# The norms of a two-layer block: weights split ahead, a fixed order of products and filler, modulation products one chunk later

## The chip, the cores and the metric

The kernel runs on one core of a Trainium2 chip. Its engines are TensorE (PE: matrix products, with PEld for its weight loads), VectorE (DVE), ScalarE (ACT), GpSimd (POOL) and SyncE (SP, which here issues the DMA loads). Each engine takes its instructions from its own queue in program order and waits at semaphores for the others. The metric is the device time of one execution in microseconds (us).

## The reference

256 tokens of width 1024 go through a first block (retention, a long convolution, a mixture of 32 experts) and then through a second block of two layers. Only the second block is touched. One layer of it is, with `rms` a root-mean-square norm over the width and six modulation vectors `sh1 ... gt2` taken from `silu(c) @ ada_w` ("ada" below):

```python
sh1, sc1, gt1, sh2, sc2, gt2 = ada_params(c, ada_w[l], ada_b[l])
h  = rms(x, g1[l]) * (1 + sc1) + sh1
u  = h @ w_in[l]               # 1024 x 2304: attention, gating, Fourier and
                               # differential-attention parts
y  = concat(fourier(u), neighbourhood_attention(u), sgu(u),
            diff_post(diff_attention(u)))   # each 256 wide, with context keys
x  = x + gt1 * (y @ w_out[l])
h  = rms(x, g2[l]) * (1 + sc2) + sh2
x  = x + gt2 * (square(relu(h @ ff1[l])) @ ff2[l])   # 1024 -> 4096 -> 1024
```

`diff_post` is a norm over each head's 64 columns. The keys and values of the context (256 tokens, computed beside the first block) also need `hc @ w_in[1]` for layer 1.

## The kernel before

Every float32 product with a large weight is done as three products of rounded halves: a weight unit of 128x1024 is split by ACT (`wh`, the rounded part) and DVE (`wl`, the rest) in `split_w` (line 277), the activations likewise (`hh`, `hl`), and PE multiplies hh by wh, hl by wh and hh by wl. `lin` (line 288) walks over a 1024x512 weight chunk in four units of two rows of tiles (k), splitting each unit just ahead of its products. A chunk lies in two buffers of 1 MB, each loaded by SP as soon as an earlier user has let the buffer go. There are seven buffers for split halves. The weights of the feed-forward come in eight chunks for `ff1` and eight for `ff2`; `ff` (line 1666) runs `ff1` of chunk c+1 before `ff2` of chunk c. After every `lin` of layer 0's feed-forward `bg_step` lets one step of "background" work in, on the modulation vectors of layer 1: two 1 MB loads of weights and 16 recorded `pada` products.

In the second block x lies transposed (`xt`). A norm is `norm_t` (line 377) and `modulated_t` (line 396): ACT squares x by pairs of tiles (`sq`), PE sums the squares with products against a column of ones (`sm,sq`), DVE takes the reciprocal root (`rq`, `sm`), PE broadcasts it over the partitions (`ident,sm`), DVE multiplies x by it (`xr`), ACT and DVE scale and shift (`hh`, `xf`) and DVE forms the rest (`hl`). Three such norms are concerned: layer 0's second norm (before its feed-forward), layer 1's first norm (computed at the end of layer 0), and layer 1's second norm. So that PE has something to do during a norm, layer 0 keeps two products of context keys back, `ctx_keys` (line 1503): 16 products `hc,w` each, whose result is copied by ACT (`ck`) and sent on. They are the "filler".

Within a layer `mixer` (line 1544) follows the string `MIX`, one letter per step: 0 to 3 are the four input projections, n and d start parts of the two attentions, b finishes the oldest started part, p is a step of the output projection `proj` (line 1595), whose last step ends with the adds into x. In layer 0 the step 0 also calls `turn` (in `layer`, line 1763), which scales x and transposes it into `xt` with 16 PE transposes and four ACT copies `x<-xt`. The last finishing step is `diff_post` (line 1466) of the last heads: a product `ones,dsq`, a reciprocal root on DVE, a copy `rb`, two transposes, a multiply (`do`) and the split `yh`. Where no order is written out by hand, a scheduler orders instructions by its own estimates; `behind` and the list `hold` pin single ones.

## Time and profile before

| what | value |
| --- | --- |
| median of 3 runs | 1798.84 us (1796.55 to 1802.67) |
| the profiled execution | 1801.79 us, its span 1800.0 us |
| mean granted clock of PE | 0.977 |
| PE busy | 1680.0 us, 93% of the span |
| DVE busy | 964.1 us, 54% |
| ACT busy | 727.0 us, 40% |
| DMA | 495.82 MB, 275 GB/s on the mean |

The second block begins at about 1092 us. Layer 0's mixer ends at 1231, its second norm lasts to 1245, its feed-forward to 1450; layer 1's first norm ends at 1463, its mixer at 1597, its second norm at 1605, its feed-forward at 1790. A busy share close to 100% says that the engine sets the time there; what is left are the stretches in which PE waits, and those in which the granted clock is 0.50, that is 1.2 instead of 2.4 GHz, where the same products take longer. In the profile a product of full float32 (filler, squares, `ones,dsq`) shows two records per instruction.

### The profile page before, as it was taken

To read this page: it belongs to the slowest core of one execution; us is meant where nothing else is said; L and a number is where in the kernel's file an instruction comes from. 1 tells how busy PE (TensorE), PEld (TensorE's weight loads), DVE (VectorE), ACT (ScalarE), POOL (GpSimd) and SP (SyncE) were. 2 spreads that over 40 slices of the span, in tenths; PEclk is the share of its full clock that TensorE was granted. 3 is DMA by queue.
4 is the path that set the end of the run, shared out by engine and by line. 5 is a ranking of instruction groups with operands and counts; after the bars stand their busy time and mean duration, and the time that the engine had idled before them with its cause. 6 is when DMAs were issued, how large, how long until landed. Compare 5 with 4: busy or idle time off the path is not lost.

```text
span 1800.0 us, 31105 instructions
## 1 busy us (share of the span) xinstructions
PE 1680.0 (93%) x12928; PEld 1323.4 (74%) x12928; DVE 964.1 (54%) x1719; ACT 727.0 (40%) x1257; POOL 62.2 (3%) x104
## 2 busy tenths in 40 slices
PE   5999999999898889999999888998999999989998
PEld 1678766668575556877677657777899987779998
DVE  5625556466224345544455466774545556755555
ACT  2413434343233333332233235563444455645443
POOL 0000000000000000000000001010000000100000
PEclk9999999999999999999999998999999999989999
DMA  9654578967699999899989995624877736235551
GB/s 372 269 211 164 225 294 324 354 243 272 277 420 420 421 396 394 319 408 420 420 350 420 403 399 162 212 96 136 299 267 257 258 126 202 80 118 188 190 189 44
DMA packets 79059, 495.82 MB, mean 275 GB/s; under 512 B 8928, under 2 KB 15744, under 8 KB 22464
## 3 DMA queue, kind: packets, MB, share of 16 engines
q1 hardware_dynamic: 74496, 478.30, 69.7%
q0 software_dynamic: 3152, 10.47, 2.0%
q10 hardware_dynamic: 1264, 4.98, 0.7%
q8 instruction: 104, 1.70, 0.4%
q14 instruction: 43, 0.35, 0.1%
HBM read 486.91 MB, written 6.82 MB: 274 GB/s over the span
## 4 chain that ended last, share of the span: by engine, by line
PE 63%; DVE 4%; ACT 3%; DMA 2%; issue 2%; DVEq 0%; ACTq 0%
PE pf L200 23%; PE pm L200 19%; PE acc L200 11%; PE pa L200 5%; PE pj L200 2%; PE pm L203 1%; DVE wl L209 1%; DMA w<-in_e 1%; PE pf L203 1%; PE pada L200 1%; DMA w<-in_ada_w 1%; ACT wh L206 0%; ACT e L206 0%; DVE sm L1320 0%; DMA w<-in_w_out 0%
## 5 line engine op out<-in xcount | busy, mean ns | idle before, releaser
L209 DVE TENSOR_TENSOR wl<-w,wh 128x1024 fp32r<-128x1024 f32 x346 | 422.9, 1225 | 421.8 <-PE pa L200 107.9
L206 ACT ACTIVATE wh<-w 128x1024 fp32r<-128x1024 f32 x346 | 362.7, 1057 | 416.6 <-PE pa L200 171.8
L200 PE MATMUL pf<-hh,wh 128*128 128x256 f32 x592 | 168.3, 286 | 4.0 <-ACT hh L206 2.3
L200 PE MATMUL pf<-hl,wh 128*128 128x256 f32 x592 | 167.1, 284 | 2.5 <-DVE hl L209 2.5
L200 PE MATMUL pf<-hh,wl 128*128 128x256 f32 x592 | 165.4, 285 | 1.6 <-DVE wl L209 1.5
L200 PE MATMUL acc<-hh,wh 128*128 128x256 f32 x512 | 143.6, 280 | 0.0
L200 PE MATMUL acc<-hl,wh 128*128 128x256 f32 x512 | 143.0, 279 | 0.0
L200 PE MATMUL acc<-hh,wl 128*128 128x256 f32 x512 | 142.9, 279 | 0.0
L200 PE MATMUL pm<-w,xg 128*32 128x256 f32 x2048 | 132.3, 390 | 2.3 <-ACT sm L206 1.2
L200 PEld LDWEIGHTS pf<-hh,wh 128*128 128x128 f32 x592 | 112.8, 191 | 8.7 <-issue 3.3
L200 PEld LDWEIGHTS pf<-hl,wh 128*128 128x128 f32 x592 | 112.7, 190 | 5.6 <-DVE hl L209 3.2
L200 PEld LDWEIGHTS pf<-hh,wl 128*128 128x128 f32 x592 | 111.8, 191 | 3.4 <-DVE wl L209 2.5
L200 PEld LDWEIGHTS pm<-w,xg 128*32 128x32 f32 x2048 | 66.7, 112 | 51.6 <-issue 13.5
L200 PEld LDWEIGHTS acc<-hh,wh 128*128 128x128 f32 x512 | 96.4, 188 | 5.9 <-ACT wh L206 5.0
L200 PEld LDWEIGHTS acc<-hh,wl 128*128 128x128 f32 x512 | 96.7, 189 | 0.0
L200 PEld LDWEIGHTS acc<-hl,wh 128*128 128x128 f32 x512 | 96.4, 188 | 0.0
L200 PE MATMUL pada<-w,csil 128*32 128x512 f32 x576 | 85.6, 625 | 9.5 <-DMA w<-in_ada_w 7.1
L200 PE MATMUL pm<-w,ex 128*32 128x256 f32 x1024 | 63.5, 388 | 16.7 <-issue 15.6
L200 PE MATMUL pm<-hh,wl 128*128 128x256 f32 x256 | 72.2, 282 | 0.0
L200 PE MATMUL pm<-hl,wh 128*128 128x256 f32 x256 | 72.2, 282 | 0.0
L200 PE MATMUL pm<-hh,wh 128*128 128x256 f32 x256 | 72.1, 282 | 0.0
L200 PE MATMUL pf<-wl,hh 128*128 128x512 f32 x160 | 65.2, 408 | 0.0
(515 smaller groups left out, 3469.9 us busy)
## 6 DMA issues: line engine op xcount, KB each, us to landing
w<-in_e SPq DMA_DIRECT2D x192, 1024.0 KB, 12.0
w<-in_ff SPq DMA_DIRECT2D x96, 1024.0 KB, 5.2
w<-in_ada_w SPq DMA_DIRECT2D x72, 1024.0 KB, 7.2
w<-in_w_in SPq DMA_DIRECT2D x54, 1024.0 KB, 7.2
w<-in_w_out SPq DMA_DIRECT2D x16, 1024.0 KB, 7.0
w<-in_ret_w_o SPq DMA_DIRECT2D x4, 1024.0 KB, 5.6
w<-in_w_su SPq DMA_DIRECT2D x3, 1024.0 KB, 4.8
adab<-in_ada_b SPq DMA_DIRECT2D x9, 256.0 KB, 12.6
```

Of the source, the lines that this page charges most:

```text
L200: return self.nc.tensor.matmul(out, lhsT, rhs, start=start, stop=stop, skip_group_check=True)
L203: return self.nc.tensor.transpose(out, in_, self.ident)
L206: return self.nc.scalar.activation(out, in_, f, **k)
L209: return self.nc.vector.tensor_tensor(out, a, b, op=op)
```

## The change

Five edits, all in the second block:

1. `ahead` splits the first two units of the weights that follow each of the three norms (`ff1` chunk 0 in both layers, the first chunk of `w_in` of layer 1) before the norm begins; `lin` takes them as ready. The DVE half of the second unit is pinned behind the last add into x, the third unit behind the last square (ACT) and behind the reciprocal root (DVE), the fourth behind the last `hl`.
2. The filler is cut into parts and each part is pinned to a place: in layer 0's second norm 3 products behind `ones,dsq` of `diff_post`, 3 behind its transposes, 4 behind the last product of squares, 6 behind the broadcast; in layer 1's first norm 4 and 12. Layer 1's second norm has none, as before.
3. The step letter `x` issues the loads of the filler and hands it to `diff_post`.
4. `turn` has a letter of its own, `t`, and runs after the projections 0, 1 and 2 instead of after 0.
5. `bg_n = -0.99, bg_rate = 1.13`: of the eight background steps in layer 0's feed-forward none runs after chunk 0, one after each of chunks 1 to 6, two after chunk 7.

```diff
-MIX = "012nndd3nbbbdndbbbvbndfdbnnsbnpbgdbdbbbbbp"
+MIX = "012nndtd3nbbbdndbbbvbndfdbnnsbnpbgdbdxbbbbbp"
...
         if self.hold:
             for later, earlier in zip(i, self.hold.pop(0)):
-                self.behind(later, earlier)
+                if earlier:
+                    self.behind(later, earlier)
         return hi, lo
 
+    def ahead(self, chunk):
+
+        self.hold = [(), (None, self.added)]
+        return chunk, [self.split_w(chunk[:, o:o + 1024]) for o in (0, 1024)]
+
     def lin(self, chunk, nk, n, jobs):
 
+        chunk, ready = chunk if isinstance(chunk, tuple) else (chunk, [])
...
-            hi, lo = self.split_w(chunk[:, u * per * n:(u + 1) * per * n])
+            hi, lo = ready[u] if u < len(ready) else self.split_w(chunk[:, u * per * n:(u + 1) * per * n])
...
-    def norm_t(self, x):
+    def norm_t(self, x, fill):
...
         rs = self.rsqrt(r, m, 2, 32.0)
+        last = self.filled(fill, last)
         p = self.ps()[:, :256]
         for t in range(2):
-            self.mm(p[:, t * P:(t + 1) * P], r[:, t:t + 1].to_broadcast([P, P]), self.ident, t == 0, True)
+            i = self.mm(p[:, t * P:(t + 1) * P], r[:, t:t + 1].to_broadcast([P, P]), self.ident, t == 0, True)
+            if t == 0 and fill:
+                self.behind(i, last)
+        self.filled(fill, i)
         return p, sq, rs
+
+    def filled(self, fill, i):
+
+        f = next(fill, None) if fill else None
+        if f:
+            self.behind(f[0], i)
+        return f[1] if f else i
...
-                if k + i == 0:
-                    self.hold = [(sq, self.added)] + [(hi, rs)] * 3
...
-            self.tt(lhs.lo[:, k:k + n, :], f, lhs.hi[:, k:k + n, :], ALU.subtract)
+            lo = self.tt(lhs.lo[:, k:k + n, :], f, lhs.hi[:, k:k + n, :], ALU.subtract)
+        self.hold = [(sq, rs), (hi, lo)]
...
+        fill = self.gap if col == 7 and not self.fill else None
+        last = self.filled(fill, i)
         r = self.rstd_of(p[:, 0:4], 4, 64.0)
...
+            if t == 0 and fill:
+                self.behind(i, last)
+        self.filled(fill, i)
...
             if step == "0":
-                self.lin(self.chunk(W[0]), 8, 512, [WJob(lhs, self.two_w(npad, nk))])
+                self.lin(w or self.chunk(W[0]), 8, 512, [WJob(lhs, self.two_w(npad, nk))])
+            elif step == "t":
                 late()
+            elif step == "x":
+                next(fill or iter(()), None)
+                self.gap = fill
...
-        lhs = self.modulated_t(xt, normed(mid), *self.mod_cols(st, self.c2("g2", 8, 8 * l), 0, 3))
-        self.bg_rate = 1.0
-        self.ff(l, xt, lhs, st[1][:, 0, 5, :])
+        w = self.ahead(self.chunk(self.a["ff1_2"][l][0]))
+        lhs = self.modulated_t(xt, self.norm_t(xt, mid), *self.mod_cols(st, self.c2("g2", 8, 8 * l), 0, 3))
+        self.bg_n, self.bg_rate = -0.99, 1.13
+        self.ff(l, xt, lhs, st[1][:, 0, 5, :], w)
         self.bg_rate = 0.0
         if not l:
-            self.norm = normed(end)
+            next(end)
+            w = self.ahead(self.chunk(self.a["w_in_2"][1][0]))
+            self.norm = self.norm_t(xt, end), w
...
-                keys = (self.ctx_keys(0, hc_d, lambda t: self.load(kv_d[1][:, :512], t.rearrange("p c k -> p (c k)"))),
-                        self.ctx_keys(1, hc_d, lambda t: self.planes(t, kd_d[1])))
+                keys = (self.ctx_keys(0, hc_d, lambda t: self.load(kv_d[1][:, :512], t.rearrange("p c k -> p (c k)")), (3, 3, 4, 6)),
+                        self.ctx_keys(1, hc_d, lambda t: self.planes(t, kd_d[1]), (4, 12)))
```

How the instructions stand before and after, at three places. A row is a line of the kernel, an operation and its tiles, out<-in, with the number of a buffer; x4 means four in a row.

PE at layer 0's second norm, before: the last output product `pj`, squares (`sm,sq`), filler (`hc,w`), broadcast (`ident,sm`), first product of the feed-forward (`hh,wh`).

```order
L200 MATMUL pj_11364<-yh_10440,wl_11708 128x256
L200 MATMUL pm_11771<-sm_11772,sq_11774 128x1 x4
L200 MATMUL pm_11816<-hc_11769,w_11767 128x256 x5
L200 MATMUL pm_11771<-sm_11772,sq_11780 128x1 x4
L200 MATMUL pm_11771<-sm_11772,sq_11786 128x1 x4
L200 MATMUL pm_11771<-sm_11772,sq_11792 128x1 x2
L200 MATMUL pm_11771<-sm_11772,sq_11796 128x1 x2
L200 MATMUL pm_11816<-hc_11769,w_11767 128x256 x11
L200 MATMUL pf_11813<-ident_81,sm_11801 128x128 x2
L200 MATMUL pf_11882<-hh_11838,wh_11884 128x256
```

The same place after the change:

```order
L200 MATMUL pj_11364<-yh_10440,wl_11719 128x256
L200 MATMUL pf_11790<-sm_11791,sq_11793 128x1 x4
L200 MATMUL pf_11790<-sm_11791,sq_11799 128x1 x4
L200 MATMUL pf_11790<-sm_11791,sq_11805 128x1 x4
L200 MATMUL pf_11790<-sm_11791,sq_11811 128x1 x2
L200 MATMUL pf_11790<-sm_11791,sq_11815 128x1 x2
L200 MATMUL pf_11569<-hc_11511,w_11509 128x256 x4
L200 MATMUL pm_11836<-ident_81,sm_11820 128x128 x2
L200 MATMUL pf_11569<-hc_11511,w_11509 128x256 x6
L200 MATMUL pf_11890<-hh_11850,wh_11782 128x256
```

The squares' products now stand together, the filler that is left stands 4 before the broadcast and 6 behind it (6 more of its 16 are further up, in `diff_post`).

DVE in the same norm, before, from the end of the reciprocal root (`sm<-rq,rq`) on:

```order
L222 SCALAR_TENSOR_TENSOR sm_11801<-rq_11803,rq_11804 128x2
L209 TENSOR_TENSOR xr_11840<-x_83,pf_11813 128x256
L219 TENSOR_SCALAR xf_11841<-xr_11840,sm_11836,adac_102 128x256
L209 TENSOR_TENSOR xr_11846<-x_83,pf_11813 128x256
L209 TENSOR_TENSOR hl_11839<-xf_11841,hh_11838 128x256
L209 TENSOR_TENSOR xr_11852<-x_83,pf_11813 128x512
L209 TENSOR_TENSOR wl_11913<-w_11878,wh_11912 128x1024
L219 TENSOR_SCALAR xf_11853<-xr_11852,sm_11836,adac_102 128x256
L209 TENSOR_TENSOR xr_11860<-x_83,pf_11813 128x512
L209 TENSOR_TENSOR hl_11839<-xf_11847,hh_11838 128x256
L209 TENSOR_TENSOR wl_11941<-w_11880,wh_11940 128x1024
L219 TENSOR_SCALAR xf_11861<-xr_11860,sm_11836,adac_102 128x256
```

After the change:

```order
L222 SCALAR_TENSOR_TENSOR sm_11820<-rq_11822,rq_11823 128x2
L209 TENSOR_TENSOR wl_11941<-w_11780,wh_11940 128x1024
L209 TENSOR_TENSOR xr_11852<-x_83,pm_11836 128x256
L219 TENSOR_SCALAR xf_11853<-xr_11852,sm_11848,adac_102 128x256
L209 TENSOR_TENSOR xr_11858<-x_83,pm_11836 128x256
L209 TENSOR_TENSOR hl_11851<-xf_11853,hh_11850 128x256
L209 TENSOR_TENSOR xr_11864<-x_83,pm_11836 128x512
L219 TENSOR_SCALAR xf_11865<-xr_11864,sm_11848,adac_102 128x256
L209 TENSOR_TENSOR xr_11872<-x_83,pm_11836 128x512
L209 TENSOR_TENSOR hl_11851<-xf_11859,hh_11850 128x256
L219 TENSOR_SCALAR xf_11873<-xr_11872,sm_11848,adac_102 128x256
L209 TENSOR_TENSOR xr_11880<-x_83,pm_11836 128x512
```

The third unit's `wl` stands in front of the first `xr`, and no other `wl` stands between the norm's own instructions.

SP's loads there, before: `ff1` chunk 0, a pair of modulation weights, `ff1` chunk 1 on both sides of the context keys' way out (`kv_d<-ck`) and of the second filler's input (`hc`), then layer 1's keys and values (`kvc`) and the next modulation pair.

```order
L225 DMA w_12009<-in_ada_w 128x2048
L225 DMA w_12011<-in_ada_w 128x2048
L225 DMA w_12027<-in_ff_2 128x2048
L225 DMA kv_d_89<-ck_11833 128x512
L225 DMA hc_13976<-hc_d 128x2048
L225 DMA w_12029<-in_ff_2 128x2048
L225 DMA kvc_14046<-kv_d_89 128x1536
L225 DMA w_12155<-in_ada_w 128x2048
L225 DMA w_12157<-in_ada_w 128x2048
L225 DMA w_12167<-in_ff_2 128x2048
```

After the change:

```order
L225 DMA w_12012<-in_ff_2 128x2048
L225 DMA w_12014<-in_ff_2 128x2048
L225 DMA w_12143<-in_ada_w 128x2048
L225 DMA w_12145<-in_ada_w 128x2048
L225 DMA kv_d_89<-ck_11845 128x512
L225 DMA hc_13976<-hc_d 128x2048
L225 DMA kvc_14058<-kv_d_89 128x1536
L225 DMA w_12155<-in_ff_2 128x2048
L225 DMA w_12157<-in_ff_2 128x2048
L225 DMA w_12273<-in_ff_2 128x2048
```

`ff1` chunk 1 stands where the first modulation pair stood, that pair stands in front of `kv_d<-ck`, and behind `kvc` come the weights of `ff2` chunk 0 (w_12155, w_12157) and not a second modulation pair. At the turn of x the 16 transposes now stand together behind the second score product after projection 2 and in front of projection 3's first product; the four copies stand on ACT behind the two exponentials that follow those scores. The instructions of POOL and of the whole first block stand as before.

## Rows read from the trace of the kernel before

**Rows 1.** waits of PE, 1222 to 1480 us: total us, times, longest

```profile
PE pa L200 <- DVE hl L209: 2.6, 3, 1.0
PE pada L200 <- DMA w<-in_ada_w: 2.6, 1, 2.6
PE pada L200 <- issue: 2.3, 1, 2.3
PE pa L200 <- ACT hh L206: 1.5, 1, 1.5
PE pf L200 <- DVE hl L209: 1.3, 1, 1.3
PE pf L200 <- ACT hh L206: 1.1, 1, 1.1
PE pj L200 <- ACT yh L206: 1.1, 1, 1.1
PE pf L203 <- DVE rb L1475: 0.6, 1, 0.6
```

**Rows 2.** busy us by stretch: PE, PEld, DVE, ACT, POOL, PEclk, DMA share, GB/s

```profile
1231.30:1238.30 7.00, 7.00 (x50) 6.57 (x49) 3.71 (x12) 2.82 (x5) 0.00 (x0) 1.00 0.00 1
1238.30:1241.70 3.40, 3.40 (x10) 2.64 (x9) 0.68 (x6) 0.00 (x0) 0.00 (x0) 0.50 0.00 0
...
1269.00:1272.40 3.40, 3.40 (x17) 2.01 (x10) 0.30 (x1) 0.00 (x0) 0.00 (x0) 0.50 1.02 424
...
1450.90:1461.40 10.50, 10.50 (x66) 9.70 (x66) 3.59 (x13) 2.14 (x4) 0.00 (x0) 1.00 0.01 2
...
1600.10:1613.80 13.70, 9.46 (x42) 8.78 (x42) 11.41 (x28) 9.06 (x16) 0.00 (x0) 0.50 0.24 79
```

**Rows 3.** timeline of PE, layer 1's first norm, its filler: start us, us, tile

```profile
1456.18 5.43 PE L200 MATMUL pf<-hc,w 128*128 128x256 f32 x24
```

**Rows 4.** timeline of PE, layer 1's second norm [idle before <-releaser]

```profile
1597.06 4.07 PE L200 MATMUL pf<-sm,sq 128*128 128x1 f32 x32
1603.02 1.22 PE L200 MATMUL pm<-ident,sm 128*128 128x128 f32 x4 [1.90 <-DVE sm L222]
...
1609.99 0.58 PE L200 MATMUL pf<-hl,wh 128*128 128x256 f32 x1 [1.20 <-DVE hl L209]
```

**Rows 5.** timeline of ACT, layer 0's second norm

```profile
1243.82 0.60 ACT L206 ACTIVATE ck<-pm 128x512 f32<-128x512 f32 x1 [9.40 <-PE pm L200]
1244.72 0.60 ACT L206 ACTIVATE hh<-xr,adac,sm 128x256 fp32r<-128x256 f32 x1 [0.30 <-DVE xr L209]
```

**Rows 6.** the page's costliest groups: count, busy us, mean ns, idle before

```profile
L209 DVE TENSOR_TENSOR wl<-w,wh 128x1024 fp32r<-128x1024 f32 x346 | 422.9, 1225 | 421.8 <-PE pa L200 107.9
```

**Rows 7.** timeline of DVE, layer 0's second norm

```profile
1252.01 0.69 DVE L209 TENSOR_TENSOR xr<-x,pf 128x512 f32<-128x512 f32 x1 [1.77 <-DMA kv_d<-ck]
```

**Rows 8.** timeline of DVE, layer 1's second norm

```profile
1604.28 0.42 DVE L209 TENSOR_TENSOR xr<-x,pm 128x256 f32<-128x256 f32 x1 [1.31 <-PE pm L200]
```

**Rows 9.** timeline of PE, the turn of x

```profile
1112.46 1.28 PE L203 MATMUL xt<-ident,x 128*128 128x128 f32 x8 [0.77 <-ACT pad L206]
1114.51 0.38 PE L200 MATMUL pa<-hh,wh 128*128 128x256 f32 x1 [0.78 <-ACT x L206]
```

**Rows 10.** timeline of PE, projection 3's first product, behind the scores

```profile
1140.95 0.58 PE L200 MATMUL pa<-wh,hh 128*128 128x512 f32 x1
```

**Rows 11.** timeline of ACT, the second exponential of those scores

```profile
1142.07 0.69 ACT L206 ACTIVATE e<-pm,sm 128x512 f32<-128x512 f32 x1 [0.52 <-DVE sm L1320]
```

**Rows 12.** timeline of PE, last chunk of layer 0's feed-forward

```profile
1426.07 1.92 PE L200 MATMUL pada<-w,csil 128*32 128x512 f32 x16
```

**Rows 13.** timeline of SP, the same chunk: issues

```profile
1407.94 17.04 SPq L225 DMA_DIRECT2D w<-in_ff  x4
```

**Rows 14.** the page's DMA issues: count, KB each, median us to landing

```profile
w<-in_ff SPq DMA_DIRECT2D x96, 1024.0 KB, 5.2
```

**Rows 15.** DMA issues, 1249 to 1271 us alone

```profile
w<-in_ff SPq DMA_DIRECT2D x3, 1024.0 KB, 14.4
```

More of the change, by code (lines that the diff above doesn't have):

```diff
@@ L130, in __init__ @@
         self.flow = ""
-        self.hold = []
+        self.hold, self.gap = [], None
         self.early, self.s8 = (), None
@@ L386, in norm_t @@
             for i, t in itertools.product(range(n), range(2)):
-                self.mm(p[:, t:t + 1], q[:, i, t * P:(t + 1) * P], one, k + i == 0 and t == 0, k + i == 7)
+                last = self.mm(p[:, t:t + 1], q[:, i, t * P:(t + 1) * P], one, k + i == 0 and t == 0, k + i == 7)
         m, r = self.sm([P, 2]), self.sm([P, 2])
@@ L1509, in ctx_keys @@
         p = self.ps().rearrange("p (m t) -> p m t", m=2)
-        for k, m in itertools.product(range(8), range(2)):
-            self.mm(p[:, m], w[:, k, m * P:(m + 1) * P], h[:, k, :], k == 0 and m == 0, k == 7)
-        o = self.t2([P, 2, 256], F32, "ck")
-        self.act(o, p)
-        put(o)
-        yield
+        todo = itertools.product(range(8), range(2))
+        for n in parts:
+            f = [self.mm(p[:, m], w[:, k, m * P:(m + 1) * P], h[:, k, :], k == 0 and m == 0, k == 7)
+                 for k, m in itertools.islice(todo, n)]
+            if n == parts[-1]:
+                o = self.t2([P, 2, 256], F32, "ck")
+                self.act(o, p)
+                put(o)
+            yield f[0], f[-1]
     def context_mixer(self, lhs, kvc, kd_d, nlam, put):
@@ L1542, in context_mixer, with mixer @@
         yield
-    def mixer(self, l, lhs, kvc, kd_d, nlam, put, proj, late):
+    def mixer(self, l, lhs, kvc, kd_d, nlam, put, proj, late, w, held, fill):
         a = self.a
@@ L1550, in mixer @@
         nk, nv, dv, dk = (own[:, i] for i in range(4))
-        bias = self.na_bias(l, self.hold[-1][1] if self.hold else None)
+        bias = self.na_bias(l, held)
         npad = self.head_pads(64)
@@ L1767, in layer @@
         cols = self.mod_cols(st, self.c2("g1", 8, 8 * l), 0, 0)
+        w = held = None
         if gains:
```

26 lines of the change are left out of this document (11 added, 15 removed).

## The prediction

> **What bounds the kernel now.** The busy shares come first: PE is busy for 93% of the span, the others for about half, so a change pays only where PE waits or where its clock is low. The second view is what PE waits for, from layer 0's `diff_post` to layer 1's first projection [rows 1]: 13.1 us in eight groups, all around norms. `diff_post` has two (0.6 for `rb`, 1.1 for `yh`), layer 0's second norm four (1.1 for `hh`, 1.3 for `hl`, then 2.3 and 2.6 in front of modulation products), layer 1's first norm two (1.5 for `hh`, 2.6 for `hl` in three pieces). The third view is the granted clock by stretch [rows 2]: it falls to 0.50, 1.2 GHz, for 3.4 us at 1238.3, for 3.4 us at 1269.0 and for 13.7 us at 1600.1; over layer 1's first norm (1450.9 to 1461.4) it stays at 1.00.
>
> The change adds no product and takes none away. PE's work stays, and the sum is made over its waits and its low-clock stretches.
>
> **`diff_post` of layer 0.** One filler product takes 5.43 / 12 = 0.45 us (24 records, two to a product) [rows 3], so three take 1.3. Three now stand behind the product that starts the wait of 0.6, three behind the transposes that start the wait of 1.1. Each covers its wait: -1.7. Beside it the early splits put two `wh` before `yh` on ACT and one `wl` before the reciprocal root on DVE. Both engines had nothing else to do there; but if the splits had to wait for a free buffer, `yh` would be late by up to the two splits. Bounds 0 and -1.7. I take -1.7: the last projection units hold four of the seven buffers, and these splits need the other three.
>
> **Layer 0's second norm.** Its four waits add up to 7.3. In the new order:
> - Root and broadcast: without filler PE waits 1.9 for the root (layer 1 [rows 4]); four filler products cover 1.8 of it. Left: 0.1.
> - `hh`: ACT copies `ck` after the last filler product and only then runs `hh`, 0.60 each [rows 5]. In the new order `ck` still stands in front, so PE waits 1.2 and some 0.2 for signals, by estimate: 1.4, where 1.1 was.
> - `hl`: on DVE no `wl` of 1.225 [rows 6] stands between the norm's instructions any more, only one in front of the first `xr`, while PE has filler. What is left of the 1.3 lies between 0 and 1.3. I take 0.5, since an `hl` still stands behind an `xr` of later tiles.
> - The 2.3: PE waited in front of a `pada` for a bank that the last `xr` was to read first, and that `xr` waited 1.77 for a DMA to empty `ck`'s buffer [rows 7]. In the new program this `xr` takes another buffer, and the `pada` is not there. Left: 0; bound 1.8, if some instruction before it met that buffer again.
> - The 2.6: this second pair of modulation weights is not wanted until a chunk later. Left: 0.
>
> Together 2.0, so -5.3 (bounds -3 and -6).
>
> **Layer 1's first norm.** The broadcast no longer waits for 12 filler products, but little comes of it: `ck` waits for them, and `hh` stands behind `ck` again. 1.5 becomes 1.4. The 2.6 for `hl` lose three `wl` splits, but DVE now multiplies the context keys (`planes`) in front of the second `hl`: I take 1.2, between 0.5 and 2.6. With 0.1 at the broadcast 4.1 becomes 2.7: -1.4 (bounds 0 and -2).
>
> **Layer 1's second norm.** It gets no filler, so its 1.9 for the root stays, and so do the waits of its `diff_post`. The 1.2 for `hl` [rows 4] goes with the `wl` splits. The third unit's `wl` now stands before the first `xr`, but there DVE waited 1.31 for the broadcast [rows 8], and the split takes 1.225 [rows 6]: covered, by 0.1. Bounds +1.2 (not covered) and -1.2; I take -1.2.
>
> **The turn of x.** Before, PE waited 0.77 for `pad` and 0.78 for the copies `x<-xt` [rows 9]. In the new place projection 3 needs the banks that the copies empty, and the copies stand behind two exponentials. The scores end at 1140.95 [rows 10], the second exponential starts at 1142.07 and lasts 0.69 [rows 11]: 1.8, and with some 0.5 for the first copy 2.3. The 16 transposes cover 1.3 to 1.7 of it (eight records took 1.28). Left is 0.6 to 1.0, where 1.55 was. Bounds +1 and -1.5; I take -0.5.
>
> **Modulation products and loads.** A `pada` group of 1.92 [rows 12] moves from one chunk to the next: 0, if the weights are there, its own and those that it displaces. The pair that stands before `kv_d<-ck` on SP waits for the last filler product, as `ck` does: no delay. `kvc` and `ff2` chunk 0 are queued behind; that is the first rival. In the last chunk two groups run, 3.8 us, and `ff2` chunk 6 takes the last two of the four load slots, the later one at 1425.0 [rows 13]. It lands 5.2 later [rows 14] and is split in 2.3: ready at 1432.5. PE, at 1426.1 [rows 12], first has 3.8 of modulation and two units; a chunk's products take (1450 - 1245 - 8 x 1.9) / 16 = 11.9, a unit 3.0. It comes to that half at 1435.9. Covered, by 3.
>
> **The clock.** The stretch at 1269.0 follows the wait of 2.6. With that wait it should go: at most half of 3.4; I take -1.5. Against it stands the order of the squares' products. From 1231.3 to 1238.3 PE is busy for all of 7.00 us and then loses its clock [rows 2]; much of that stretch was squares' products, of one column each. At layer 1's first norm they stood in two pieces with filler between, and the clock stayed at 1.00. Now all stand together in both norms, as in layer 1's second norm (4.07 us [rows 4], at 0.50 from its end on). I leave one short stretch in layer 0's norm, as it is, and add one in layer 1's first: +1.5.
>
> The Trainium skill, "TensorE: Matmul & The Clock Gate", Part 1: The HAM clock gate, has the half rate follow idleness of PE and the full rate sustained busyness. By that rule alone squares' products that keep PE busy cost no clock, the 1.5 just added falls away, and the sum would be -11.6. The trace speaks against it, with PE fully busy ahead of the fall at 1238.3.
>
> **Sum**: -1.7 - 5.3 - 1.4 - 1.2 - 0.5 - 1.5 + 1.5 = -10.1. The profiled execution took 1801.8, so its like would take 1791.7. It lies 3 above the median of the runs, 1798.8; against that the forecast is 1788.7.
>
> **Rivals.**
> 1. *The gain is given back in the loads.* From 1249 to 1271 loads of feed-forward weights took 14.4 on the median to land [rows 15]. `ff2` chunk 0 is now requested behind `kvc`, which waits for `ck`'s way out: before, from `ck`'s end at 1244.4 [rows 5] to 1252.0 [rows 7], 7.6. `ck` ends some 2.6 earlier, because six filler products (2.7) went into waits; so the request falls at 1249.4. At 14.4 it lands at 1263.8 and is split at 1266. PE starts the feed-forward at about 1242.4 (the end of the first `hh`, 1245.3, less 2.6 and the 0.3 that it waited) and needs it after two chunks and a `pada` group, at 1268. A margin of 2. Should it take 18, PE waits 2, and as much or more for the second half: with 5 lost, 1794. For it: the wait of 2.6 was for such a load. Against: `ff1` chunk 1, 2 MB, is no longer in that queue.
> 2. *Slower: the clock.* If the contiguous squares bring to both norms at the ends of layer 0's feed-forward a stretch like that of 13.7, each costs up to 6.9, together 13.7, of which 3.0 are in the time already: +10.7, so 1799.4, above the median before. It decides from about 13 us each. For it: layer 1's second norm has the same order. Against: there PE was busy for 9.46 of the 13.7 only [rows 2]; here filler follows.
> 3. *The early splits don't come early.* If ACT's splits wait for buffers in front of `yh`, the 1.7 of `diff_post` stay, the adds to x come 1 later in both layers, and the gain of layer 1's first norm goes with it: 5 lost, 1794.
>
> **How the numbers follow.** The forecast (1784 to 1792.5) has 0.68, the first rival 0.13, the third 0.09, the second 0.06, others 0.04. About 0.3%, 5.4 us, is what a measurement of this kernel can tell from no change, so faster means under 1793.4. Nearly all of the forecast lies there and some 0.4 of the first and third rivals: faster 0.77, same 0.18, slower 0.05. Low end, 1783.5: no new clock stretch (-1.5), layer 1's long one shorter by 3.4 once its 1.2 is gone (-1.7), less left at `hl` and the turn (-2). High end, 1796: the first or third rival with nothing won at the turn and in layer 1's norms.
>
> **What would show it.** Right: no PE wait over 0.3 in layer 0's `diff_post`; about 1.4 for `hh` at the norms on either side of layer 0's feed-forward, none in front of the first two `pada` groups; no 1.2 for `hl` in layer 1's second norm; the clock at 1.00 around 1265. Wrong: PE waits for `w<-in_ff` in `ff2` chunk 0 or in the last chunk, stretches at 0.50 of well over 4 us behind the squares, or `yh` late behind `wh`.

## The result, and the profile after

The changed kernel took 1780.18 us (median, 1778.65 to 1783.12), the kernel before 1797.69 on the same chip: 17.5 less, a ratio of 0.990 with a 95% interval of 0.9878 to 0.9923. The forecast was 1788.7, with a range from 1783.5 to 1796.0. The direction was right, the gain was 17.5 where 10.1 were forecast, and the time lies 3.3 below the low end.

The profiled execution took 1783.1 us (span 1781.4). PE is busy for 1673.6 us (94%), DVE for 963.9, ACT for 727.3, at a mean granted clock of 0.977 as before. The gain therefore does not show in the mean clock, and the busy shares say little about it. The waits do.

First the waits of PE around the norms on both sides of layer 0's feed-forward, which answer to [rows 1] (us in total, times, longest):

```profile
PE pf L200 <- ACT hh L206: 1.2, 1, 1.2
PE pa L200 <- ACT hh L206: 1.2, 1, 1.2
PE pa L200 <- DVE hl L209: 0.8, 1, 0.8
PE pf L200 <- DVE hl L209: 0.6, 1, 0.6
```

Eight groups with 13.1 us have become four with 3.7. `rb` and `yh` of `diff_post` are gone, and so are both waits in front of `pada`. What is left is one `hh` and one `hl` for each norm. (`rb` and `yh` would stand a little before 1222 us in this profile; there is no such wait from 1095 us on either.)

Next, busy time and granted clock by stretch (busy us and count of PE, PEld, DVE, ACT, POOL, then PEclk), which answers to [rows 2]:

```profile
1221.70:1228.70 7.00, 7.00 (x58) 6.67 (x56) 5.45 (x13) 3.64 (x8) 0.00 (x0) 1.00 0.01 2
1228.70:1235.50 6.80, 6.80 (x23) 5.98 (x24) 3.15 (x15) 0.33 (x1) 0.00 (x0) 0.50 0.49 155
1255.00:1275.00 20.00, 20.00 (x172) 18.43 (x172) 11.62 (x13) 9.94 (x12) 0.00 (x0) 1.00 0.89 348
1433.30:1440.30 7.00, 7.00 (x60) 6.94 (x59) 3.36 (x8) 2.40 (x5) 0.00 (x0) 1.00 0.07 26
1440.30:1443.70 3.40, 3.40 (x12) 2.85 (x11) 2.35 (x10) 0.00 (x0) 0.00 (x0) 0.51 0.00 0
1583.70:1593.90 10.20, 7.15 (x32) 6.77 (x33) 7.62 (x24) 4.60 (x10) 0.00 (x0) 0.50 0.31 104
```

The stretch at half clock around 1269 is gone (third row: 1.00 throughout). A new one of 3.4 stands at layer 1's first norm, at 1440.3, and in the 7.00 us before it PE was busy all the time. The one at layer 0's second norm lasts 6.8 here. Layer 1's long one is down from 13.7 to 10.2.

The turn of x on PE, which answers to [rows 9], and on ACT (start us, us, instruction, idle before and its releaser):

```profile
1131.88 0.59 PE L200 MATMUL pf<-own,pad 128*128 128x256 f32 x2
...
1134.46 1.91 PE L203 MATMUL xt<-ident,x 128*128 128x128 f32 x16
1136.71 0.50 PE L200 MATMUL pa<-wh,hh 128*128 128x512 f32 x1 [0.34 <-ACT x L206]
```

```profile
1135.39 0.69 ACT L206 ACTIVATE e<-pm,sm 128x512 f32<-128x512 f32 x1 [0.52 <-DVE sm L1337]
1135.98 0.19 ACT L206 ACTIVATION_READ_ACCUMULATOR e<-pm,sm 128x1 f32 x1
1136.07 2.05 ACT L206 ACTIVATE x<-xt 128x512 f32<-128x512 f32 x4
```

The copies do stand behind the second exponential, as the forecast had it; but the 16 transposes cover 1.91 of that, and 0.34 is left of 1.55.

Layer 1's second norm on PE, which answers to [rows 4]:

```profile
1581.17 4.51 PE L200 MATMUL pf<-sm,sq 128*128 128x1 f32 x32
1587.58 1.23 PE L200 MATMUL pm<-ident,sm 128*128 128x128 f32 x4 [1.90 <-DVE sm L222]
1589.95 0.58 PE L200 MATMUL pf<-hh,wh 128*128 128x256 f32 x1 [1.15 <-ACT hh L206]
```

The wait of 1.20 for `hl` is gone; 1.90 for the root and 1.15 for `hh` stay.

All of it by stage, from the first product of layer 0's first projection to the end of the span. Each number is a mean over two profiles of each kernel (the two repeats are among the experiments). "Waits" are the gaps between PE's records in the stage, added up, and the gap in front of its first product, as the 1.2 to 1.5 for a first `hh`, is counted with it; "half" is the time at a granted clock of 0.50.

| stage | us before, after | waits before, after | half before, after |
| --- | --- | --- | --- |
| layer 0's mixer, with the turn | 129.2, 125.4 | 6.7, 4.1 | 7.4, 5.8 |
| its last `diff_post` to the end of the second norm | 21.9, 20.6 | 1.7, 0.0 | 5.1, 6.8 |
| its feed-forward (from the first `hh` of the norm) | 205.7, 197.0 | 7.2, 1.7 | 3.4, 0.0 |
| layer 1's first norm | 12.6, 13.9 | 0.0, 0.0 | 0.0, 3.4 |
| layer 1's mixer (from the first `hh`) | 124.8, 122.5 | 7.7, 5.6 | 0.0, 0.0 |
| its last `diff_post` | 8.6, 8.6 | 1.7, 1.7 | 3.4, 3.4 |
| its second norm and feed-forward | 190.7, 188.4 | 4.2, 3.1 | 13.7, 10.2 |
| the end | 12.4, 11.9 | 0.0, 0.0 | 8.9, 3.1 |
| sum | 705.8, 688.2 | 29.3, 16.2 | 41.9, 32.8 |

The sum falls by 17.6, as the medians do. Waits give 13.1 of it. A stretch at half clock costs at most half its length, so 9.1 us less of them gives up to 4.6. The first block, which the change leaves alone, ended between 1089.5 and 1095.5 in the profiles taken, so single profiles can't be compared by their spans to better than some 5 us.

### The profile page after: what moved, and what is told of

The parts are those of the page before. It is cut to its first block, busy times and chain, and to the rows that moved or that the text cites. A ratio compares the mean times of both kernels' runs of the same rounds, so it can differ in the third digit from the quotient of the medians.

```text
span 1781.4 us, 31112 instructions
## 1 busy us (share of the span) xinstructions
PE 1673.6 (94%) x12928; PEld 1319.8 (74%) x12928; DVE 963.9 (54%) x1719; ACT 727.3 (41%) x1257; POOL 63.0 (4%) x104
## 4 chain that ended last, share of the span: by engine, by line
PE 65%; DVE 4%; ACT 3%; issue 2%; DMA 1%; DVEq 0%; ACTq 0%
PE pf L200 24%; PE pm L200 19%; PE acc L200 11%; PE pa L200 5%; PE pj L200 2%; PE pm L203 1%; DMA w<-in_e 1%; PE pf L203 1%; PE pada L200 1%; DVE wl L209 1%; ACT e L206 0%; DVE sm L1337 0%; DMA w<-in_w_out 0%; ACT wh L206 0%; ACT eh L206 0%
## 6 DMA issues: line engine op xcount, KB each, us to landing
w<-in_e SPq DMA_DIRECT2D x192, 1024.0 KB, 12.4
adab<-in_ada_b SPq DMA_DIRECT2D x9, 256.0 KB, 12.6
```

## The experiments

The theory before them: what the forecast counted came as forecast, and what it missed lies in the turn of x. Its rival: the missing 7 us are in the norms and in the loads, or come from the clock by chance. Later the question was what the remaining waits and stretches hang on.

### The turn alone, and everything but the turn

On the kernel before (`turn_alone`), and the other way round on the changed kernel (`all_but_turn`: `t` put directly behind `0`):

```diff
-MIX = "012nndd3nbbbdndbbbvbndfdbnnsbnpbgdbdbbbbbp"
+MIX = "012nndtd3nbbbdndbbbvbndfdbnnsbnpbgdbdbbbbbp"
...
+            elif step == "t":
                 late()
```

```diff
-MIX = "012nndtd3nbbbdndbbbvbndfdbnnsbnpbgdbdxbbbbbp"
+MIX = "0t12nndd3nbbbdndbbbvbndfdbnnsbnpbgdbdxbbbbbp"
```

> The kernel before with edit 4 alone (the turn of x after projections 0, 1, 2). Theory A (the turn was under-priced: besides the two waits of 0.77 and 0.78 its new place takes the wait of 1.44 in front of the product pm<-pt,own at 1162.7, because ACT's splits of the next weights no longer stand in front of the copy pt): 3.3 us faster than before in the stretch from the first product of projection 0 to the score product near 1200 (104.9 us before), total about -3.3. Rival B (the turn is worth the 0.5 forecast, and the rest of the -3.3 in that stretch comes with the other edits): -0.5, and the wait of 1.44 is still there. The start of the second block (1095.5 before) tells of chance: theory A has it anywhere within some 3 us, whatever the kernel.

> The changed kernel with the turn back behind projection 0 (edits 1, 2, 3 and 5). Theory A: 3.3 us slower than the changed kernel, so about 14 faster than before; the waits 0.77, 0.78 and 1.44 are back. Rival B: within 1 us of the changed kernel.

Measured: `turn_alone` 1790.51 against 1798.37, ratio 0.9957 (0.9942 to 0.9973); `all_but_turn` 1783.30, ratio 0.9913 (0.9896 to 0.9930). By its ratio the turn alone is worth 5 to 10 us on the kernel before, more than the 3.3 of theory A. Taken out of the changed kernel it costs 3.1 by the medians, as theory A has it, though the intervals of the two ratios (0.9913 without it, 0.990 with it) overlap. Layer 0's mixer took 125.2 us in `turn_alone` (129.2 before) and 128.2 in `all_but_turn` (125.4 in the changed kernel), with 4.1 and 6.5 of waits. The rest of what `turn_alone` gained lies behind the mixer: in its profile the second `pada` waits 0.5 and not 2.6, and layer 0's second norm has no half clock. The repeat further down shows how little of that lasts. Waits of PE in that mixer in `all_but_turn`:

```profile
PE pm L200 <- ACT pt L206: 1.2, 1, 1.2
PE xt L203 <- ACT pad L206: 0.8, 1, 0.8
PE pf L203 <- ACT pt L206: 0.8, 1, 0.8
PE pa L200 <- ACT x L206: 0.8, 1, 0.8
```

The two waits of [rows 9] are back, and with them a third, `pm` for `pt` (ACT's copy of the transposed exponentials `e`), some 50 us further on, which the forecast never looked at. (`pf` for `pt` stands in all these kernels.) The third is 1.44 in the kernel before. There, on ACT and PE:

```profile
1157.83 2.01 ACT L206 ACTIVATE wh<-w 128x1024 fp32r<-128x1024 f32 x2 [2.10 <-DMA w<-in_w_out]
1159.74 0.67 ACT L206 ACTIVATE e<-pf,sm 128x512 f32<-128x512 f32 x1
1160.31 0.19 ACT L206 ACTIVATION_READ_ACCUMULATOR e<-pf,sm 128x1 f32 x1
1160.40 0.68 ACT L206 ACTIVATE e<-pm,sm 128x512 f32<-128x512 f32 x1
1160.97 0.20 ACT L206 ACTIVATION_READ_ACCUMULATOR e<-pm,sm 128x1 f32 x1
1161.06 0.59 ACT L206 ACTIVATE pt<-pm 128x512 f32<-128x512 f32 x1
```

```profile
1162.72 1.08 PE L200 MATMUL pm<-pt,own 128*64 128x256 f32 x4 [1.44 <-ACT pt L206]
```

And ACT in the changed kernel:

```profile
1152.40 1.07 ACT L206 ACTIVATE wh<-w 128x1024 fp32r<-128x1024 f32 x1 [0.37 <-DMA w<-in_w_out]
1153.37 0.57 ACT L206 ACTIVATE pt<-pm 128x512 f32<-128x512 f32 x1
```

Before, two splits of the output weights wait 2.10 for their load with `e` and `pt` queued behind them; in the changed kernel the scheduler puts `pt` behind one split that waits 0.37. Moving the turn shifted that order too.

### The order around `pt` alone

`splits_behind_pt`, on the kernel before: the second and third of those splits in layer 0 are pinned behind the first and second copy to `pt`.

```diff
+        pins = [None, 0, 1]
...
+                if l == 0 and pins:
+                    at = pins.pop(0)
+                    if at is not None:
+                        self.behind(self.halves[0], self.pts[at])
```

> The kernel before, with nothing changed but two of ACT's splits of output weights in layer 0 pinned behind the first and second copies pt (they stood in front of the exponentials, waiting 2.1 us for a load of w_out). Theory A (the wait of 1.44 in front of pm<-pt,own is ACT's queue held up by those splits, and the turn's move took it by putting them later): the wait goes and layer 0's mixer (129.2 us, mean of two profiles) is 1.4 shorter with the turn where it was. Rival (the wait needs the turn out of the way): it stays at 1 or more.

Measured: 1796.67 against 1798.33, ratio 0.9995 (0.9983 to 1.0007): no difference that can be measured, and a gain of 1 is within the interval. The wait fell from 1.44 to 0.19:

```profile
1158.20 1.08 PE L200 MATMUL pm<-pt,own 128*64 128x256 f32 x4 [0.19 <-ACT pt L206]
```

Two others came behind it, 0.22 and 0.41 for later copies `pt`. The waits of the mixer fell from 6.7 to 5.7, 0.3 of it in front of its first product, which the edit does not touch. The profiled run spent 8.3 us of that mixer at half clock and took 128.9. So theory A holds for the wait, and its 1.4 in the stage did not come. What the turn brings in waits is 1.2 at the turn and 1.4 at `pt`, 2.6 together, by the table of the result. The rest of the stage's 3.8 is not a wait: 1.6 us less at half clock (7.4 to 5.8, worth up to 0.8), and 0.4 that was not placed. In the repeats below the time at half clock in this mixer runs from 2.9 to 8.6 in kernels with the same order there, so that part is chance.

### The modulation products alone, and everything but these

`modulation_alone` on the kernel before, `all_but_modulation` on the changed one (with `0.0, 1.0`):

```diff
-        self.bg_rate = 1.0
+        self.bg_n, self.bg_rate = -0.99, 1.13
```

> The kernel before with edit 5 alone (modulation products one chunk later). The forecast puts the waits of 2.3 and 2.6 in front of pada and the low-clock stretch at 1269 to this edit: if that holds alone, about -5 to -6.4 us. Rival: the 2.3 belongs to the xr that waits for the DMA of ck, and comes back as a wait for hl behind that xr; then only 2.6 + 1.5 = 4.1 go, or less.

> The changed kernel with the background steps as before (one after every chunk from chunk 0 on). If edit 5 alone carries the waits in front of pada: a wait for w<-in_ada_w of 2 to 5 us comes back in chunk 0 or 1, and the kernel is 3 to 6 us slower than the changed one. Rival: the other edits (another buffer for xr, ff1 chunk 1 earlier) had taken these waits, then it is within 1 us of the changed kernel.

Measured: 1790.11, ratio 0.9949 (0.9932 to 0.9966), and 1786.49, ratio 0.9932 (0.9915 to 0.9949). The first gains 8.3 by the medians, more than either theory allows; layer 0's feed-forward gives 5.3 of it (205.7 to 200.4), and the rest was not placed. The second is 6.3 slower than the changed kernel by the medians. In `all_but_modulation` the product waits for its load again (PE), and the clock falls at 1254.2, in that wait, for 6.8:

```profile
1254.77 1.94 PE L200 MATMUL pada<-w,csil 128*32 128x512 f32 x8 [3.03 <-DMA w<-in_ada_w]
```

Layer 0's feed-forward takes 203.1 there and 197.0 in the changed kernel: a wait of 3.0 and a stretch behind it that costs up to 3.4. In `modulation_alone` both `pada` waits are gone, but a new one of 2.2 for `hl` has come, behind this on DVE:

```profile
1247.06 0.69 DVE L209 TENSOR_TENSOR xr<-x,pf 128x512 f32<-128x512 f32 x1 [1.15 <-DMA kv_d<-ck]
```

It is the `xr` of [rows 7], still waiting for `ck`'s buffer. The forecast's "takes another buffer" holds only together with the other edits; by itself this edit turns one wait, the 2.3, into another.

### The early splits, and the filler in `diff_post`

`no_early_splits`: `ahead` only hands on the chunk, and the pins of the kernel before stand again. `filler_in_norm_only`: none in `diff_post`, 4 products before the broadcast and 12 behind it.

```diff
-        self.hold = [(), (None, self.added)]
-        return chunk, [self.split_w(chunk[:, o:o + 1024]) for o in (0, 1024)]
+        return chunk, []
...
+                if k + i == 0:
+                    self.hold = [(sq, self.added)] + [(hi, rs)] * 3
...
-        self.hold = [(sq, rs), (hi, lo)]
```

```diff
-                self.gap = fill
+                self.gap = None
...
-                keys = (self.ctx_keys(0, hc_d, lambda t: self.load(kv_d[1][:, :512], t.rearrange("p c k -> p (c k)")), (3, 3, 4, 6)),
+                keys = (self.ctx_keys(0, hc_d, lambda t: self.load(kv_d[1][:, :512], t.rearrange("p c k -> p (c k)")), (4, 12)),
```

> The changed kernel with the weight units split as before (no unit ahead of the norm, splits between the norm's instructions), filler order, turn and modulation as changed. Theory A: the early splits carry the waits for hl: 0.7 at layer 0's second norm, 1.8 at layer 1's first, 1.2 at layer 1's second with 3.4 us more at half clock there (1.7): about 5 us slower than the changed kernel. Rival: these waits are set by xr and xf on DVE, and the splits only fill holes: within 2 us of the changed kernel.

> The changed kernel with no filler in diff_post; the first filler is cut 4 and 12 around the broadcast of layer 0's second norm. Theory A: the waits 0.6 and 1.1 in diff_post come back, and the two stretches at half clock change by chance only: 1.7 us slower. Rival (the 6.8 us at half clock at 1228.7 in the changed kernel come from filler moved out of the norm, so that squares stand alone): the stretch shrinks to 3.4 and gives 1.5 back, so the sum is 0.

Measured: 1786.98 against 1797.95, ratio 0.9940 (0.9924 to 0.9956), and 1783.89, ratio 0.9914 (0.9900 to 0.9928). By the medians they are 6.8 and 3.7 slower than the changed kernel; the second is not resolved by the ratios. Waits of PE from 1222 to 1480 us in `no_early_splits`, against the four rows of the result:

```profile
PE pa L200 <- DVE hl L209: 2.6, 2, 1.6
PE pf L200 <- DVE hl L209: 2.4, 2, 1.4
...
```

The two rows for `hh` stay at 1.2, and one of 0.6 for the root is new. So the early splits, with their pins, are what shortens the `hl` waits: 5.0 without them, 1.4 with them, and 1.2 more in layer 1's second norm. In `filler_in_norm_only` the waits of [rows 1] in `diff_post` come back, seen here from 1095 to 1222 us:

```profile
PE pj L200 <- ACT yh L206: 1.0, 1, 1.0
...
PE pf L203 <- DVE rb L1494: 0.6, 1, 0.6
```

`yh` and `rb` were covered by the six products, and by nothing else.

### `ck` behind `hh`

The forecast said that `hh` would wait behind `ck`. In `ck_behind_hh` (on the changed kernel) `ck` is pinned behind the second `hh` of the norm:

```diff
...
-            if n == parts[-1]:
-                o = self.t2([P, 2, 256], F32, "ck")
-                self.act(o, p)
-                put(o)
             yield f[0], f[-1]
+        hi = self.hh1
+        o = self.t2([P, 2, 256], F32, "ck")
+        self.behind(self.act(o, p), hi)
+        put(o)
+        yield
...
```

> The changed kernel with ACT's copy ck pinned behind the second hh in the two norms around layer 0's feed-forward. Theory A (hh waits because ck waits for the last filler product): the wait of 1.17 in front of the first hh product shrinks to some 0.1 at both norms, about 2 us faster than the changed kernel. Rival (the wait only moves to hl, which needs xf behind ck): the 1.17 go, 0.5 to 1 of each comes back in front of hl, below 1 us faster.

Measured: 1777.72 against 1797.95, ratio 0.9894 (0.9876 to 0.9912); the changed kernel's was 0.990, so the gain of some 2 us is not resolved by the ratios. The waits are: of the four rows from 1222 to 1480 us one is left.

```profile
PE pa L200 <- DVE hl L209: 0.6, 1, 0.6
```

On ACT, `hh` no longer waits for the filler products:

```profile
1231.69 0.60 ACT L206 ACTIVATE hh<-xr,adac,sm 128x256 fp32r<-128x256 f32 x1 [4.67 <-DVE xr L209]
1232.47 0.60 ACT L206 ACTIVATE hh<-xr,adac,sm 128x256 fp32r<-128x256 f32 x1 [0.18 <-DVE xr L209]
1234.33 0.60 ACT L206 ACTIVATE ck<-pf 128x512 f32<-128x512 f32 x1 [1.25 <-PE pf L200]
```

That step is shown: both waits of 1.2 were `ck`, and they did not come back in front of `hl`. At layer 1's first norm the gain is given back in this profile, where the stretch at half clock lasted 6.8.

### Filler in layer 1's second norm

`idle_filler_layer1` adds work: 9 products whose result nobody reads, cut into parts of 1, 2, 4 and 2 at the places of layer 0's filler.

```diff
+    def idle_keys(self, k, parts):
+        yield
+        p = self.ps()
+        for n in parts:
+            f = [self.mm(p[:, :256], self.ident, k[:, j % 2, :], True, True) for j in range(n)]
+            yield f[0], f[-1]
...
-                                None if l else gains, *((None,) * 2 if l else keys))
+                                None if l else gains, *((self.idle_keys(kvc[:, 0], (1, 2, 4, 2)), None) if l else keys))
```

> The changed kernel with nine needless products (kvc by ident, 128x256, results unused) pinned into layer 1's waits: one and two in diff_post (waits 0.61 and 1.04), four before and two behind the broadcast of its second norm (waits 1.90 and 1.15). Theory A (PE's idleness there, not the squares, drops the clock): the stretches at half clock of 3.4 at 1577 and 10.2 at 1584 shrink or go, and the kernel is 2 to 6 us faster than the changed one. Rival (the squares' one-column products drop it): the stretches stay, and the products cost 0 to 1.

Measured: 1779.77, ratio 0.9890 (0.9874 to 0.9906), against 0.990 for the changed kernel. Busy time and granted clock by stretch there:

```profile
1577.80:1584.80 7.00, 6.82 (x58) 6.66 (x58) 4.86 (x12) 3.66 (x8) 0.00 (x0) 1.00 0.00 0
1584.80:1588.20 3.40, 3.40 (x10) 2.69 (x10) 2.63 (x12) 0.00 (x0) 0.00 (x0) 0.51 0.90 308
1588.20:1598.40 10.20, 9.57 (x73) 8.65 (x72) 8.52 (x16) 8.98 (x15) 0.00 (x0) 1.00 0.01 2
```

At half clock stand 3.4 us there and not the changed kernel's 3.4 and 10.2, with the squares' products together as before. So the filler around them counts here, and theory A's stretches shrank; its 2 to 6 us did not come. The waits from layer 1's last `diff_post` through its feed-forward go from 4.7 to 1.1, and the three stages take 194.7, where they took 196.8 in the changed kernel's first profile: a gain of 2.1. Waits gave 3.6 and the clock up to 5.1; the filler's own nine products took back some 4 (at 0.45 each [rows 3]), and the rest was not placed. In the median the 2.1 do not show.

### The two kernels once more

`before_again` and `after_again` are the two kernels unchanged, for a second profile of each.

> The kernel before, one more profiled execution. If the 2.4 us by which the changed kernel was ahead at the start of the second block are chance: the first product of projection 0 starts anywhere from 1091 to 1096 us here (1095.5 in the first profile), and the total is nearer to the median of 1798 than the first profile's 1801.8. If they belong to the change: 1095.5 again. The wait in front of the second pada group (2.56) and the stretches at half clock near 1238 and 1269: the same again if the kernel sets them, others if chance does.

> The changed kernel, one more profiled execution. If the stretches at half clock behind the squares' products (6.8 at 1229, 3.4 at 1440) are set by the order of the products, they are there again, at the same place to within 3 us; if they are chance, at least one is gone.

Measured: 1800.7 and 1784.8 us, one run each. The first product of projection 0 starts at 1091.9 in the kernel before (1095.5 in its first profile) and at 1095.0 in the changed one (1093.1): where the second block starts is chance. Waits and stretches of the changed kernel repeat to 0.2 us. Those of the kernel before repeat but for the wait in front of its first `pada`, 1.7 and not 2.3, and for the stretches of 3.4: one at 1110.7 and one at 1226.8 are new. So a stretch or two of 3.4, up to 1.7 us each, is chance at least.

### The squares in two pieces, and the best versions

`squares_in_two_pieces` (on the changed kernel) puts four filler products between two halves of the squares' products, in both norms that have filler:

```diff
+                if k == 4 and fill and i == t == 0:
+                    self.behind(i_, last)
...
+            if k == 2:
+                last = self.filled(fill, last)
```

`ck_and_idle_filler` joins the edits of `ck_behind_hh` and `idle_filler_layer1`; `all_three` adds the two pieces to it, in layer 1's second norm too.

> The changed kernel with four filler products pinned between the squares' products of the two norms around layer 0's feed-forward (two pieces, as before the change), the rest of the filler around the broadcast. Theory A (squares standing together bring the half clock): no stretch at half clock near 1440, the one near 1229 at most 3.4; 1 to 3 us faster than the changed kernel. Rival (the stretches cost next to nothing, because the one-column products take as long at either clock): the stretch near 1440 goes, the time stays within 1 us.

> The changed kernel with both of ck behind the second hh and the needless products in layer 1's waits. Theory A (the two act at different places and add up): hh's waits of 1.17 gone at both norms, no wait over 0.4 in layer 1's second norm, 4 to 6 us faster than the changed kernel. Rival (the gain of one is chance of the clock): no more than 2.5 faster.

> The changed kernel with all three: squares in two pieces with filler between in the two norms around layer 0's feed-forward (in layer 1's second norm with two needless products between), ck behind the second hh, needless products in layer 1's waits. Theory A (waits and low-clock stretches add up): 2 to 4 faster than without the pieces, about 1771. Rival (without hh's waits the squares no longer matter): within 1 of the kernel without the pieces (1774).

Measured: 1775.60, ratio 0.9872 (0.9855 to 0.9888); 1774.17, ratio 0.9872 (0.9853 to 0.9890); 1776.01, ratio 0.9878 (0.9863 to 0.9894). By the medians that is 4.6, 6.0 and 4.2 below the changed kernel; the intervals overlap with its own (0.9878 to 0.9923), and the three can't be told from one another. Order and clock of `squares_in_two_pieces` at layer 1's first norm:

```profile
1433.33 1.84 PE L200 MATMUL pf<-sm,sq 128*128 128x1 f32 x16
1435.04 1.97 PE L200 MATMUL pm<-hc,w 128*128 128x256 f32 x8
1436.85 1.84 PE L200 MATMUL pf<-sm,sq 128*128 128x1 f32 x16
1438.55 1.97 PE L200 MATMUL pm<-hc,w 128*128 128x256 f32 x8
```

```profile
1222.00:1242.00 20.00, 18.09 (x126) 16.18 (x125) 14.36 (x39) 10.70 (x22) 3.32 (x4) 1.00 0.45 137
1430.00:1450.00 20.00, 17.98 (x122) 16.11 (x121) 10.69 (x28) 8.16 (x16) 0.66 (x1) 1.00 0.12 48
```

With the same products, and waits as in the changed kernel, neither norm has a stretch at half clock; layer 0's second norm takes 10.2 where it took 13.1, layer 1's first 12.6 where it took 13.9. That is the price of a stretch behind contiguous squares, 1.3 to 2.9 a norm. It is not always paid: `all_but_modulation` and `no_early_splits` have the squares of layer 0's second norm together too, no stretch in it, and take 10.2 and 10.6 there. `ck_and_idle_filler` has the lowest median of the kernels tried; its second block takes 678.9 us by the stages of the table, with 9.8 of waits. `all_three` has no half clock between 1100 and 1762, but a stretch of 12.2 at its very end, and is no faster: 1.8 slower by the medians, where theory A had 2 to 4 faster.

### Repeats of the two single edits

`turn_alone_again` and `modulation_alone_again`, unchanged, for a second profile of each.

> The kernel with edit 4 alone, one more profile. Theory A (of its gain of 8 only the 4 in layer 0's mixer belong to it, the rest were low-clock stretches and a shorter wait for modulation weights in one execution): mixer 125 again, but the second norm or the feed-forward of layer 0 up to 3 longer than in the first profile (12.3 and 203.8). Rival: 12.3 and 203.8 again, so the gain there belongs to the turn as well.

> The kernel with edit 5 alone, one more profile. If the order of loads sets the gain: layer 0's feed-forward takes 200 to 201 again (205.7 before), with one wait of 2.2 in front of hl, which is the last xr waiting for ck's buffer. If it is chance: more than 1.5 off.

Measured: 1788.4 and 1788.3 us, one run each. Layer 0's mixer took 124.4 with the turn moved and 126.9 without, with waits of 3.8 and 6.7. Behind the mixer, theory A holds in part for the turn: the second norm lasts 14.0 and not 12.3, with a stretch of 3.4, and the second `pada` waits 2.6 again. The feed-forward takes 203.8 both times (once with a wait of 0.5 and a stretch of 3.4, once with the wait of 2.6 and no stretch), 1.9 less than before; that 1.9 stays open. With edit 5 alone the feed-forward takes 200.4 and 200.6, with a wait for `hl` of 2.2 and 2.6: that gain repeats. In `turn_alone_again` layer 1's long stretch was 6.8 and not 13.7, with no edit there: its length is a matter of chance by some 7 us, too. The two single edits give 7.9 and 8.3 us by their first medians, and cost 3.1 and 6.3 when they are taken out of the changed kernel; the whole change gives 17.5. So what an edit is worth depends on the rest of the kernel, or on chance, by up to some 5 us.

## Why the prediction was wrong

The direction, and most terms of the sum, came out. By its own steps, forecast and measured (waits by the table, or by the rows of the result):

| step | forecast | measured |
| --- | --- | --- |
| `diff_post` of layer 0 | -1.7 | -1.7 |
| layer 0's second norm | -5.3 | -5.5 |
| layer 1's first norm | -1.4 | -2.1 |
| layer 1's second norm, `hl` | -1.2 | -1.2 |
| the turn of x | -0.5 | -2.6 |
| the clock: stretch at 1269 gone, a new one at layer 1's first norm | 0.0 | -1.7 and +1.4 |
| the clock elsewhere: layer 0's mixer -0.8, its second norm +0.9, layer 1's long stretch -1.7, the end -0.5 | 0 | -2.1, much of it chance |
| not placed | 0 | -2.1 |
| sum | -10.1 | -17.6 |

**The step that failed is "The turn of x ... I take -0.5", bounds +1 and -1.5.** The mechanism at its place was right, the size was not: 0.34 is left there, because the transposes cover 1.91 and not 1.3 to 1.7. That is 1.2 gained at the turn where 0.5 was taken. The larger miss is that the step looked at the turn alone. Moving it changed ACT's order some 50 us further on, where two splits stood in front of `pt`, waiting 2.10 for their load. That wait of 1.44 was in the trace of before, outside the stretch read for [rows 1]. `all_but_turn` brings all three waits back, `turn_alone` takes them away; `splits_behind_pt` shows that the third hangs on the splits in front of `pt` (1.44 to 0.19); there 0.6 came back in two later waits, and nothing showed in the median. The step is 2.1 of the 7.5 us that the forecast missed; 2.1 more is the clock outside the sum, 2.1 was not placed, and the rest are small terms.

**The clock is the second miss, and only in part a step.** Both stretches that the sum named came as named, with the sizes named: the one at 1269 went with its wait (and is back, at 6.8, in `all_but_modulation`, behind a wait of 3.0), and the new one follows the contiguous squares (gone in `squares_in_two_pieces`). The link to the wait is not strict: `turn_alone_again` has a wait of 2.6 and no stretch in that feed-forward. By the rule of the Trainium skill ("TensorE: Matmul & The Clock Gate", Part 1: The HAM clock gate) that sustained work keeps the full rate, the new one should not be there. The measurement decides against it here, with PE busy for 7.00 of 7.00 us before the fall at 1440.3; that is busy as the profile shows it, where the ends of products are modelled. What the sum left out: layer 1's long stretch is 10.2 and not 13.7 in both profiles of the changed kernel, up to -1.7, which the forecast had put into its low end only. The wait of 1.2 for `hl` went at the same time, but `turn_alone_again` and `splits_behind_pt` have 6.8 with that wait in place, so the link was not shown. It is likely all the same: the six other profiles with that wait have 13.7, and all seven without it and without needless products there have 10.2. The shorter stretch at the end (8.9 to 3.1) changed its stage by 0.5 only, and that stage varies by 1.6 over the profiles of the experiments. Most of what was not placed, 1.5, lies in the first feed-forward, which is 8.7 shorter: 5.5 by waits, up to 1.7 by the stretch.

**Layer 1's first norm** was mis-sized by 0.7: 0.8 is left for `hl` where 1.2 was taken, 1.2 for `hh` where 1.4, and none at the broadcast where 0.1. A reading of the forecast was loose, too: in layer 1's second norm the clock falls at 1600.1 [rows 2], 1 us before the squares end, and not "from its end on".

**What was right.** `hh` behind `ck`: 1.2 at both norms, forecast 1.4 (`ck_behind_hh`); the 0.2 that the forecast added for signals came from no row, and did not show. The filler covers `rb` and `yh` (`filler_in_norm_only`). The early splits come early and clear DVE for `hl` (`no_early_splits`). The first rival, loads, did not happen: there is no wait for `w<-in_ff`; the first half of `ff2` chunk 0 landed 12.9 after its issue, where 14.4 would have left a margin of 2. The second rival needed about 13 at both norms; the stretches there were 6.8 and 3.4. The third needed the waits of `diff_post` to stay, and these are zero. One of the forecast's own signs of being wrong did come: the stretch behind layer 0's squares is 6.8, well over 4. It cost up to 0.9 only, since the kernel before has 5.1 there on the mean.

**The range** was too narrow below. Its low end took the sum's terms for exact and added three favourable extras of 1.5 to 2; the turn alone was out by 2.1, and the chance part of the clock, some 2 to 3 us, had no place in it. Two profiles of the kernel before would have shown this spread.

## What to carry to other kernels

When an edit moves work in an engine's queue, read the waits over the whole stage that is rescheduled, not only at the place of the edit: an instruction that waits for its load holds all that is queued behind it, and that order changes with everything ahead of it. Split the time of the bounding engine into waits, time at the lower clock and the rest, by stage, and do it for two profiles of the same kernel before trusting a difference of a few us. Filler that covers waits and also parts long rows of very small products took the half clock out of the norms here; what that is worth in the median was not resolved.

## What the hardware showed that was not expected

- Half clock behind contiguous one-column products. Of nine profiles of kernels whose squares stand together at layer 1's first norm, eight show a stretch of 3.4 or 6.8 in that norm (the ninth is `ck_and_idle_filler`); of nine with filler between the squares, none does. At layer 0's second norm it is seven of nine with all 32 records of the squares in a row, five of seven with 24 in a row (the order before the change), and none of two with 16 and 16. A stretch can come elsewhere, too: in both profiles with edit 5 alone one of 3.4 stands just behind layer 1's first norm, after its waits of 1.5 and 0.9.
- Filler that computes nothing useful shortens the time at half clock: in layer 1's second norm 13.6 us (two stretches) became 3.4, at the price of the filler's own time, and the stages gained 2.1, in one profile.
- Loads at some 250 GB/s with the DMA engines busy. While POOL's four 256 KB loads `nab<-in_na_rpb` (13.4 us each on the median to landing) run, the core moves some 250 GB/s; after them, over 400. The rate in 40 slices of 1245 to 1260 us of the changed kernel, and the issues in that stretch:

```profile
GB/s 295 262 175 295 273 251 273 208 284 229 273 219 251 246 197 126 246 180 257 317 180 322 218 235 213 251 284 224 246 317 410 371 437 415 415 437 393 459 393 415
...
w<-in_ff SPq DMA_DIRECT2D x3, 1024.0 KB, 12.4
kvc<-kv_d SPq DMA_DIRECT2D x1, 768.0 KB, 11.7
```

The DMA engines are busy for nearly all of both parts, so the busy share does not tell the one from the other. The three 1 MB loads issued there took 12.4 us on the median to land; over the whole run the median is 5.0. The Trainium skill ("DMA: Bandwidth & Descriptors", Queues, rings and completion order) says that each DMA engine takes turns between the queues that have work for it, packet by packet. The rows agree so far as both queues use the engines in that stretch: SP's (q1) for 77.2% of their time and POOL's (q0) for 24.2%. That POOL's four loads are the cause of the low rate was not tried.
